# Gate and up products of the second layer's FFN as seven products of quarters, with sums of quarters on VectorE and GpSimd

## The chip, the cores and the metric

The kernel runs on one core of a Trainium2 chip. TensorE multiplies, VectorE (DVE), ScalarE (ACT) and GpSimd (POOL) work on tiles in SBUF and PSUM, and SyncE (SP) issues the DMAs. The metric is the device time of one execution in microseconds, median of the runs shown.

## The reference

Two layers of a backbone over 1024 latent tokens (and 256 context tokens in the first), width 1024, in float32. Each layer mixes tokens in two ways (A and B, then C and D), and then runs a feed-forward part (FFN) on the normed tokens:

```python
def swiglu(h, w_gate, w_up, w_down):
    return (jax.nn.silu(h @ w_gate) * (h @ w_up)) @ w_down
...
        x = x + g_m * y
        x = x + g_f * swiglu(modulate(rmsnorm(x, norm_ffn_w[i]), sh_f, sc_f), ffn_w_gate[i], ffn_w_up[i], ffn_w_down[i])
```

The hidden width is 2816. A last rmsnorm gives the output. The change concerns `h @ w_gate` and `h @ w_up` of the second layer, for 1024 tokens.

## The kernel before

Float32 precision comes from three products of rounded operands: `split` (L54) makes a high part (a CAST on ScalarE, L56) and a low part (a subtraction on VectorE or GpSimd, L57), and `mm3` (L46) multiplies high by high, high by low, low by high into one PSUM bank, lines L49, L50, L51. Every matmul here is 128 x 128 weights by 512 tokens.

Tokens lie along the free axis: eight tiles `xT` of 128 channels by 1024 tokens hold x, and `mixc`, `mixd` hold the normed h, one high and one low tile for each of the eight depths. Tokens are taken in two blocks of 512 (`XBLK`).

Before the FFN, `out_proj` (L389) multiplies the mixed heads by the output weights, block by block, in four groups of two channel tiles (`op`), and `residual` (L312, one VectorE operation at L316) adds them to x. Behind each block, `rstd` (L264) squares x on ScalarE, sums on VectorE (`sqacc`, L275), sums over partitions on TensorE (`ss`, L279) and takes the root (`rv`, with a power on GpSimd, L249); `spread` (L253) makes a diagonal and spreads it by a matmul (`rbc`, L261); `norm` (L283) scales each channel tile (`nt`, L295), adds the shift and splits it, the odd tiles with GpSimd (L299 to L301), the even ones without (L303, L304).

`ffn` (L327) goes over 22 tiles of 128 hidden columns. `up` multiplies h by a gate tile and an up tile for one block (`pg`, `pu`, both named pg in the profile: 8 depths x 3 matmuls each), takes silu on ScalarE (L345), multiplies on VectorE (L346) and splits the hidden values. `down` takes two hidden tiles and multiplies them by the down weights into eight channel tiles and two blocks (`dn`, 16 x 6 matmuls), each added to x by `residual`. Down runs two tiles behind up. Weights come by DMA in slabs of 512 KB and are split (`wslab`, L60).

PSUM has eight banks. `psum` (L70) hands out tag "s" as halves of a tile of two banks, two such tiles in turn; the first and the second half of one tile go to two products that follow each other. The framework holds a writer of the second half back until the readers of the first half that stand ahead of it in the program are done. The down products of layer 2 use the four single banks of tags t, t, m and o.

The order of instructions on each engine is fixed when the kernel is built, by the framework's scheduler; pools with a number of buffers decide when a tile can be written again. At the end, `final` (L1294) norms each token, and the output is stored.

Of the kernel before, what the change touches and what calls it, by code (L numbers as in the profile page):

```python
# [53 lines left out]
def split(s, hi, lo, src, eng="act"):  # L54

    s.nc.scalar.copy(hi, src)  # L56
    (s.nc.gpsimd if eng == "pool" else s.nc.vector).tensor_tensor(lo, src, f32(hi), ALU.subtract)  # L57
# [12 lines left out]
def psum(s, tag, name=None):  # L70

    if tag != "s":
        return s.ps.tile([P, 512], F32, name=name or tag, tag=tag, bufs=2 if tag == "t" else 1)
# [187 lines left out]
    s.nc.tensor.matmul(bc[:, :n * P], s.ones, dg, start=True, stop=True)  # L261


def rstd(s, xT, blk, add=None):  # L264

    nc = s.nc
    o, n = blk
    acc = s.np_.tile([P, 512], F32, name="sqacc", tag="sqacc", bufs=2)
    for k in range(KT):
        if k == 0:  # L270
            nc.scalar.activation(acc[:, :n], xT[0][:, o:o + n], AF.Square)
        else:
            sq = s.np_.tile([P, 512], F32, name="sq", tag="sq", bufs=2)
# [1 line left out]
            (add or nc.vector).tensor_tensor(acc[:, :n], acc[:, :n], sq[:, :n], ALU.add)  # L275
# [1334 lines left out]
```

## Time and profile before

| what | value |
|---|---|
| median of 3 runs | 2867.76 us (2862.70 to 2868.23) |
| profiled execution | 2863.98 us, its span 2862.0 us |
| TensorE busy in the span | 2758.1 us, 96% |
| VectorE, ScalarE, GpSimd busy | 1551.5, 892.2, 196.5 us |
| last matmul of out_proj starts at | 2120.05 us |
| first gate product of layer 2 starts at | 2121.35 us |

A row of the timeline gives the start and the duration in us, the engine, the line of the kernel, the operation, what it writes and reads, and in brackets how long the engine was idle ahead of it and what ended that. Matmuls overlap in the pipeline, so a row of 0.39 us does not mean that the next starts 0.39 us later. PEld is the loading of weights. A row of a window gives its bounds and length, then busy time and number of instructions of PE, PEld, DVE, ACT and POOL, then the granted TensorE clock, the DMA share and GB/s.

### The profile page before, as it was taken

How to read it: one execution, taken by the hardware profiler on the slowest of the kernel's cores; microseconds unless marked ns; L12 is line 12 of the kernel's file. 1: busy time of each engine (PE TensorE's matmuls, PEld its weight loads, DVE VectorE, ACT ScalarE, POOL GpSimd, SP SyncE). 2: the span in 40 equal slices, each digit the busy share in tenths (PEclk: the TensorE clock that was granted, in tenths of full speed). 3: DMA queues.
4: the chain of work that ended last, by engine and by line, in shares of the span. 5: the costliest groups of instructions: out<-in, count | busy, mean ns of one | idle time of the engine just before them, and what ended most of it. 6: DMA issues, size and time to landing. Idle time of an engine off the chain costs nothing.

```text
span 2862.0 us, 38369 instructions
## 1 busy us (share of the span) xinstructions
PE 2758.1 (96%) x14927; PEld 2339.4 (82%) x14927; DVE 1551.5 (54%) x2791; ACT 892.2 (31%) x1899; POOL 196.5 (7%) x233
## 2 busy tenths in 40 slices
PE   8999999899999999999999998998999999999998
PEld 3889888777888888888888787787878888888887
DVE  4655677676664544645533466756673333333435
ACT  3432566554411111111111145654251111111112
POOL 0000222121100000000000020312010000000000
PEclk9999999999999999999999999999999999999999
DMA  8545655674231322313310143533631111111111
GB/s 302 169 129 154 183 156 171 207 215 129 70 115 59 97 65 61 103 39 95 89 37 30 46 148 100 164 118 102 213 101 52 45 45 52 52 45 52 52 45 67
DMA packets 285686, 298.50 MB, mean 104 GB/s; under 512 B 33416, under 2 KB 228673, under 8 KB 285505
## 3 DMA queue, kind: packets, MB, share of 16 engines
q1 hardware_dynamic: 285505, 296.06, 34.3%
q8 instruction: 118, 1.93, 0.3%
q14 instruction: 63, 0.52, 0.1%
HBM read 228.09 MB, written 64.49 MB: 102 GB/s over the span
## 4 chain that ended last, share of the span: by engine, by line
PE 79%; DVE 9%; DMA 5%; ACT 4%; issue 3%; POOL 1%; SPq 0%; DVEq 0%; ACTq 0%; POOLq 0%
PE pg L51 12%; PE pg L50 12%; PE pg L49 12%; PE dn L49 5%; PE dn L50 5%; PE dn L51 5%; PE o L750 2%; PE pt L720 1%; DMA adaw<-in_ada_w_dram 1%; DVE xT L316 1%; DVE adaacc L183 1%; DVE wlo L57 1%; PE ho L49 1%; PE sp L661 1%; PE qk L49 1%
## 5 line engine op out<-in xcount | busy, mean ns | idle before, releaser
L56 ACT CAST whi<-wraw 128x1024 fp32r<-128x1024 f32 (+2 forms) x186 | 188.4, 1014 | 676.4 <-PE dn L50 404.0
L316 DVE SCALAR_TENSOR_TENSOR xT<-dn,mod,xT 128x512 f32<-128x512 f32 (+1 forms) x448 | 299.7, 686 | 122.4 <-PE dn L51 120.3
L57 DVE TENSOR_TENSOR wlo<-wraw,whi 128x1024 fp32r<-128x1024 f32 (+2 forms) x186 | 220.7, 1189 | 238.2 <-ACT whi L56 236.4
L49 PE MATMUL dn<-hhi,whi 128*128 128x512 f32 (+1 forms) x896 | 328.6, 368 | 6.3 <-DVE xT L316 4.7
L50 PE MATMUL dn<-hlo,whi 128*128 128x512 f32 (+1 forms) x896 | 326.9, 365 | 0.0
L51 PE MATMUL dn<-hhi,wlo 128*128 128x512 f32 (+1 forms) x896 | 326.5, 365 | 0.0
L51 PE MATMUL pg<-hh,wlo 128*128 128x512 f32 x688 | 269.2, 391 | 0.6 <-DVE wlo L57 0.6
L49 PE MATMUL pg<-hh,whi 128*128 128x512 f32 x688 | 269.0, 391 | 0.0
L346 DVE TENSOR_TENSOR sg<-sg,pg 128x512 f32<-128x512 f32 (+1 forms) x110 | 69.3, 630 | 367.6 <-ACT sg L345 367.5
L50 PE MATMUL pg<-hl,whi 128*128 128x512 f32 x688 | 268.3, 390 | 0.0
L183 DVE SCALAR_TENSOR_TENSOR adaacc<-adaw,cs,adaacc 128x1024 f32<-128x1024 f32 x140 | 175.0, 1280 | 117.7 <-DMA adaw<-in_ada_w_dram 114.9
L345 ACT ACTIVATE sg<-pg 128x512 f32<-128x512 f32 (+1 forms) x110 | 60.6, 551 | 547.0 <-PE pg L51 547.0
L49 PEld LDWEIGHTS dn<-hhi,whi 128*128 128x128 f32 x896 | 168.9, 189 | 39.6 <-DVE xT L316 11.1
L51 PEld LDWEIGHTS dn<-hhi,wlo 128*128 128x128 f32 x896 | 168.9, 189 | 27.0
L50 PEld LDWEIGHTS dn<-hlo,whi 128*128 128x128 f32 x896 | 169.0, 189 | 26.3
L51 PEld LDWEIGHTS pg<-hh,wlo 128*128 128x128 f32 x688 | 129.5, 188 | 28.4 <-DVE wlo L57 1.5
L50 PEld LDWEIGHTS pg<-hl,whi 128*128 128x128 f32 x688 | 129.5, 188 | 26.0
L49 PEld LDWEIGHTS pg<-hh,whi 128*128 128x128 f32 x688 | 129.5, 188 | 25.9
L49 PE MATMUL pg<-mixc,whi 128*128 128x512 f32 x344 | 133.9, 389 | 0.9 <-DVE xT L316 0.9
L50 PE MATMUL pg<-mixd,whi 128*128 128x512 f32 x344 | 134.3, 390 | 0.0
L51 PE MATMUL pg<-mixd,wlo 128*128 128x512 f32 x344 | 133.8, 389 | 0.0
L50 PE MATMUL pg<-mixc,whi 128*128 128x512 f32 x344 | 133.8, 389 | 0.0
(569 smaller groups left out, 6198.7 us busy)
## 6 DMA issues: line engine op xcount, KB each, us to landing
adaw<-in_ada_w_dram SPq DMA_DIRECT2D x96, 512.0 KB, 3.9
wraw<-in_ffn_w_gate_dram SPq DMA_DIRECT2D x44, 512.0 KB, 3.7
wraw<-in_ffn_w_up_dram SPq DMA_DIRECT2D x44, 512.0 KB, 3.8
wraw<-in_ffn_w_down_dram SPq DMA_DIRECT2D x44, 512.0 KB, 3.8
wraw<-in_ab_w_in_dram SPq DMA_DIRECT2D x20, 512.0 KB, 6.3
xd<-xT SPq DMA_DIRECT2D x16, 640.0 KB, 6.1
xs<-xd SPq DMA_DIRECT2D x32, 256.0 KB, 3.2
xd<-xs SPq DMA_DIRECT2D x32, 256.0 KB, 2.9
```

The lines of the kernel that those rows point to most:

```text
L49: nc.tensor.matmul(out, wh, xh, start=start, stop=False)
L50: nc.tensor.matmul(out, wh, xl, start=False, stop=False)
L51: nc.tensor.matmul(out, wl, xh, start=False, stop=stop)
L56: s.nc.scalar.copy(hi, src)
L57: (s.nc.gpsimd if eng == "pool" else s.nc.vector).tensor_tensor(lo, src, f32(hi), ALU.subtract)
L183: nc.vector.scalar_tensor_tensor(acc[:, v], w, c, acc[:, v], ALU.mult, ALU.add)
L316: s.nc.vector.scalar_tensor_tensor(xT[k][:, o:o + n], ps, s.mod[l][:, 8 * vec + k, sel:sel + 1], xT[k][:, o:o + n], ALU.mult, ALU.add)
L345: nc.scalar.activation(sg[:, :n], pg[:, :n], AF.Silu)
L346: nc.vector.tensor_tensor(sg[:, :n], sg[:, :n], pu[:, :n], ALU.mult)
L661: nc.tensor.matmul(sp[:, o:o + n], qq[:, x, :], kk[:, t0:t0 + n], start=x == 0, stop=x == 1)
L720: nc.tensor.transpose(pt[:n, jj * P:(jj + 1) * P], y[:, c:c + n], s.ident)
L750: nc.tensor.matmul(o_ps[:, ba * P:bz * P], vv[:n, kt, :], at(x, sl)[:n, 0, ba:bz, :].rearrange("p b q -> p (b q)"), start=q == 0 and x == ...
```

## The change

Take h as four quarters: A11 is block 0 with the first four depths, A12 block 0 with the last four, A21 and A22 the same of block 1. Take the weights of two neighbouring hidden tiles as quarters B11, B12, B21, B22 (depth half by tile). Then the four quarters of the product come from seven products:

- sums of h: s1 = A21 + A22, s2 = s1 - A11, s3 = A11 - A21, s4 = A12 - s2, made once. `norm_first` keeps A11 and A11 + A12 in float32, and `norm_second`, the norm of block 1, makes the sums depth by depth.
- sums of weights: t1 = B12 - B11, t2 = B22 - t1, t3 = B22 - B12, and B21 - t2, made on GpSimd for each pair of tiles (`quarters`, L490); all seven are split.
- products (`quad`): 1 = A11 B11, 2 = A12 B21, 5 = s1 t1, 6 = s2 t2, 7 = s3 t3, 3 = s4 B22, 4 = A22 (B21 - t2), each of 4 depths x 3 matmuls.
- sums of products: c11 = 1 + 2; u = 1 + 6; c12 = u + 5 + 3; u + 7; c22 = u + 7 + 5; c21 = u + 7 + 4. Products 1 and 5 are copied from PSUM by ScalarE (L531, L536), 2, 6, 7, 3, 4 are added by VectorE (L533, L535, L539, L543, L546), and two sums of SBUF tiles are on GpSimd (L538, L541).

`ffn_sums` runs gate, then up, then down for each pair of hidden tiles, with down directly behind its pair. The weights' pool is closed and opened anew ahead of the FFN, with units of 4 x 128 columns; the pool of `norm_second`'s scratch is closed there, and the buffers `hu` of `quad` lie in its memory. The final norm's tiles come from a pool that takes the place of the sums.

```diff
-        norm(s, xT, hT, l, 1, blk, rstd(s, xT, blk), True)
+        behind(blk)
...
+        out_proj(s, a["cd_w_out"][0], mix, xT, 1, XBLK, [0, 1, 2, 3], S.places(),
+                 lambda blk: (norm_first if blk == XBLK[0] else norm_second)(s, xT, hT, S, 1))
...
-        ffn(s, a, 1, xT, hT, XBLK, TAIL, final(s, s.np_, a, xT, out))
+    wps.close()
+    with R("wp2") as s.wp, R("fp2") as s.fp:
...
+        ffn_sums(s, a, 1, xT, hT, S, tail)
```

The norm of block 1 with the sums, L455 to L478 (`normed` scales on VectorE, L431, and adds the shift on ScalarE, L432):

```python
    for k in range(4):
        a21, a22 = scratch(s), scratch(s)
        normed(s, xT, k, blk, bc, l, a21)
        normed(s, xT, k + 4, blk, bc, l, a22)
        s1 = sum_(nc.vector, a21, a22, ALU.add)
        s2 = sum_(nc.vector, s1, S.a11[k], ALU.subtract)
        s3 = sum_(nc.gpsimd, S.a11[k], a21, ALU.subtract)
        s4 = sum_(nc.gpsimd, S.a1s[k], s1, ALU.subtract)
        for i, v, eng in ((6, s2, "dve"), (5, s1, "dve"), (7, s3, "pool"), (3, s4, "dve"), (4, a22, "pool")):
            parts(i, k, v, eng)
```

The weights, L503 to L513, where `parts` splits a unit, and the products, L530 to L547, of which `out` names the place and `done` is silu for gate, multiplication (L572) and split for up:

```python
    sub(t, t, b11)
    parts(1, b11)
    parts(2, b21)
    parts(5, t)
    sub(t, b22, t)
    parts(6, t)
    sub(b21, b21, t)
    sub(t, t, b11)
    parts(7, t)
    parts(3, b22)
    parts(4, b21)
...
    u, v = room(), room()
    nc.scalar.copy(u, product(1))
    c = out(0, 0, None)
    add(c, product(2), u, ALU.add)
    done(0, 0, c)
    add(u, product(6), u, ALU.add)
    nc.scalar.copy(v, product(5))
    c12 = out(0, 1, None)
    nc.gpsimd.tensor_tensor(c12, u, v, ALU.add)
    add(u, product(7), u, ALU.add)
    c = out(1, 1, v)
    nc.gpsimd.tensor_tensor(c, u, v, ALU.add)
    done(1, 1, c)
    add(c12, product(3), c12, ALU.add)
    done(0, 1, c12)
    c = out(1, 0, u)
    add(c, product(4), u, ALU.add)
    done(1, 0, c)
```

How the instructions move is shown at three places. The first is TensorE at the norm of block 1 (ss and rbc are its two sums). Before, they stand within the gate products of the first tile:

```order
L50 MATMUL pg<-mixd,whi 128x512
L51 MATMUL pg<-mixd,wlo 128x512
L49 MATMUL pg<-mixd,whi 128x512
L279 MATMUL ss<-ones,sqacc 128x1 x4
L50 MATMUL pg<-mixd,whi 128x512
L51 MATMUL pg<-mixd,wlo 128x512
L49 MATMUL pg<-mixd,whi 128x512
L50 MATMUL pg<-mixd,whi 128x512
L51 MATMUL pg<-mixd,wlo 128x512
```

After, product 1 (mixc) ends, then come both, and directly behind them product 6, whose operands s_19651, s_19678 and two more are s2 of the four depths:

```order
L51 MATMUL qp<-mixc,wlo 128x512
L279 MATMUL ss<-ones,sqacc 128x1 x4
L261 MATMUL rbc<-diag,ones 128x512
L49 MATMUL qp<-s_19651,whi 128x512
L50 MATMUL qp<-s_19651,whi 128x512
L51 MATMUL qp<-s_19651,wlo 128x512
L49 MATMUL qp<-s_19678,whi 128x512
L50 MATMUL qp<-s_19678,whi 128x512
L51 MATMUL qp<-s_19678,wlo 128x512
```

So no product stands beside the sums: the 12 matmuls of product 1 are ahead of ss, and product 2, which needs nothing of block 1, stands behind product 6.

The second place is VectorE and GpSimd in the norm of block 1. VectorE before, from its first scaling on (L295, nt are scaled tiles, mixc the low parts at L304):

```order
L295 SCALAR_TENSOR_TENSOR nt_19630<-xT0_19241,acol11_182,rbc_19626 128x512
L295 SCALAR_TENSOR_TENSOR nt_19634<-xT1_19242,acol11_182,rbc_19626 128x512
L304 SCALAR_TENSOR_TENSOR mixc_18359<-nt_19630,mod1_178,mixc_18358 128x512
L295 SCALAR_TENSOR_TENSOR nt_19639<-xT2_19243,acol11_182,rbc_19626 128x512
L295 SCALAR_TENSOR_TENSOR nt_19643<-xT3_19244,acol11_182,rbc_19626 128x512
L304 SCALAR_TENSOR_TENSOR mixc_18799<-nt_19639,mod1_178,mixc_18798 128x512
L346 TENSOR_TENSOR sg_19745<-sg_19745,pg_19696 128x512
```

VectorE after, depth 0 and the beginning of depth 1 (nt_19637 and nt_19638 are a21 and a22 of depth 0, nt_19643 is s1, nt_19645 s2, nt_19649 s4; L463 are sums, L57 low parts):

```order
L431 SCALAR_TENSOR_TENSOR nt_19637<-xT0_19241,acol11_182,rbc_19633 128x512
L431 SCALAR_TENSOR_TENSOR nt_19638<-xT4_19245,acol11_182,rbc_19633 128x512
L463 TENSOR_TENSOR nt_19643<-nt_19637,nt_19638 128x512
L463 TENSOR_TENSOR nt_19645<-nt_19643,s30_19438 128x512
L57 TENSOR_TENSOR mixc_18359<-nt_19643,mixc_18358 128x512
L431 SCALAR_TENSOR_TENSOR nt_19664<-xT1_19242,acol11_182,rbc_19633 128x512
L57 TENSOR_TENSOR s20_19651<-nt_19645,s20_19651 128x512
L57 TENSOR_TENSOR s40_19659<-nt_19649,s40_19659 128x512
L431 SCALAR_TENSOR_TENSOR nt_19665<-xT5_19246,acol11_182,rbc_19633 128x512
L463 TENSOR_TENSOR nt_19670<-nt_19664,nt_19665 128x512
L463 TENSOR_TENSOR nt_19672<-nt_19670,s31_19439 128x512
```

GpSimd in the same stretch had only the low parts of four odd tiles before; after, a depth reads:

```order
L57 TENSOR_TENSOR mixd_18286<-nt_19638,mixd_18285 128x512
L463 TENSOR_TENSOR nt_19647<-s30_19438,nt_19637 128x512
L463 TENSOR_TENSOR nt_19649<-s40_19442,nt_19643 128x512
L57 TENSOR_TENSOR s30_19656<-nt_19647,s30_19656 128x512
L57 TENSOR_TENSOR mixd_18288<-nt_19665,mixd_18287 128x512
L463 TENSOR_TENSOR nt_19674<-s31_19439,nt_19664 128x512
```

The scaling of a22 of depth 1 (nt_19665) has come to stand behind the low part of s4 of depth 0 (s40_19659), which needs GpSimd's third operation of that depth.

The third place is TensorE inside a pair of tiles, at gate's products 7, 4 and 3. Before, at the border of two tiles (pg_20240 is the up product of block 1, pg_20308 the PSUM tile that gate and up of the next tile's block 0 share, matmul by matmul):

```order
L49 MATMUL pg_20240<-mixd_18291,whi_20182 128x512
L50 MATMUL pg_20240<-mixd_18292,whi_20182 128x512
L51 MATMUL pg_20240<-mixd_18291,wlo_20183 128x512
L49 MATMUL pg_20308<-mixc_18358,whi_20298 128x512
L50 MATMUL pg_20308<-mixc_18359,whi_20298 128x512
L51 MATMUL pg_20308<-mixc_18358,wlo_20299 128x512
L49 MATMUL pg_20308<-mixc_18358,whi_20304 128x512
L50 MATMUL pg_20308<-mixc_18359,whi_20304 128x512
L51 MATMUL pg_20308<-mixc_18358,wlo_20305 128x512
```

After, in the third pair of tiles (qp_20743 is a PSUM tile of two banks with product 7 in its first half and product 3 in its second, qp_20775 the next one):

```order
L49 MATMUL qp_20743<-s33_19737,whi_20671 128x512
L50 MATMUL qp_20743<-s33_19737,whi_20671 128x512
L51 MATMUL qp_20743<-s33_19737,wlo_20672 128x512
L49 MATMUL qp_20775<-mixd_18285,whi_20679 128x512
L50 MATMUL qp_20775<-mixd_18286,whi_20679 128x512
L51 MATMUL qp_20775<-mixd_18285,wlo_20680 128x512
L49 MATMUL qp_20775<-mixd_18287,whi_20679 128x512
L49 MATMUL qp_20743<-s40_19659,whi_20675 128x512
L50 MATMUL qp_20743<-s40_19659,whi_20675 128x512
L51 MATMUL qp_20743<-s40_19659,wlo_20676 128x512
```

A product that had begun ran to its end before, alone or with its partner; now four matmuls of product 4 have come to stand between the end of product 7 (s33) and the beginning of product 3 (s40), which writes the second half of product 7's tile. The other products of a pair lie in the same way: another product's first 4 to 6 matmuls, then the second half.

More of the change, by code (lines that the diff above doesn't have):

```diff
@@ L261, in spread, with rstd @@
     s.nc.tensor.matmul(bc[:, :n * P], s.ones, dg, start=True, stop=True)
-def rstd(s, xT, blk, add=None):
+def rstd(s, xT, blk, add=None, tag=None, bufs=2):
     nc = s.nc
     o, n = blk
-    acc = s.np_.tile([P, 512], F32, name="sqacc", tag="sqacc", bufs=2)
+    acc = s.np_.tile([P, 512], F32, name="sqacc", tag=tag or "sqacc", bufs=bufs)
     for k in range(KT):
@@ L386, in ffn, with __init__, new, places @@
     down(HT - 2, hs[HT - 2:])
-def out_proj(s, w, mix, xT, hT, l, blocks, order, places):
+class Sums:
+    def __init__(self, pool):
+        self.pool = pool
+        self.s = {}
+    def new(self, tag, shape=(P, 2, 512), dt=F32R):
+        return self.pool.tile(list(shape), dt, name=tag, tag=tag, bufs=1)
+    def places(self):
+        for i in (0, 2):
+            yield [self.new(f"s2{i + x}", (P, 4, 2 * P)) for x in range(2)]
+    def first(self):
+        return [[self.new(f"s{i}{k}", dt=F32)[:, 0, :] for k in range(4)] for i in (3, 4)]
+    def operand(self, hT, i, k):
+        if i in (6, 7, 3):
+            tag = f"s{ {6: 2, 7: 3, 3: 4}[i]}{k}"
+            if tag not in self.s:
+                self.s[tag] = self.new(tag)
+            return self.s[tag][:, 0, :], self.s[tag][:, 1, :]
+        k0, o = {1: (0, 0), 2: (4, 0), 4: (4, 512), 5: (0, 512)}[i]
+        return [hT[k0 + k][x][:, o:o + 512] for x in range(2)]
@@ new lines, with scratch, normed, spread_rstd @@
+SCRATCH = 8
+def scratch(s):
+    return s.np_.tile([P, 512], F32, name="nt", tag="nt", bufs=SCRATCH)
+def normed(s, xT, k, blk, bc, l, dst):
+    o, n = blk
+    s.nc.vector.scalar_tensor_tensor(dst, xT[k][:, o:o + n], s.acol[l][1][:, k, 0:1], bc[:, :n], ALU.mult, ALU.mult)
+    s.nc.scalar.activation(dst, dst, AF.Identity, bias=s.mod[l][:, 24 + k, 0:1])
+def spread_rstd(s, xT, blk):
+    r = rstd(s, xT, blk, None, "nt", SCRATCH)
+    bc = psum(s, s.nbanks[1], "rbc")
+    spread(s, s.np_, r, bc, "nt", SCRATCH)
+    return bc
@@ new lines, in norm_first, with norm_second, sum_, parts @@
+def norm_first(s, xT, hT, S, l):
+    blk = XBLK[0]
+    bc = spread_rstd(s, xT, blk)
+    S.a11, S.a1s = S.first()
+    for k in range(KT):
+        v = (S.a11 if k < 4 else S.a1s)[k % 4]
+        normed(s, xT, k, blk, bc, l, v)
+        split(s, hT[k][0][:, :512], hT[k][1][:, :512], v, "pool" if k % 2 else "dve")
+        if k >= 4:
+            s.nc.gpsimd.tensor_tensor(v, v, S.a11[k - 4], ALU.add)
+def norm_second(s, xT, hT, S, l):
+    nc = s.nc
+    blk = XBLK[1]
+    bc = spread_rstd(s, xT, blk)
+    def sum_(e, x, y, op):
+        out = scratch(s)
+        e.tensor_tensor(out, x, y, op)
+        return out
+    def parts(i, k, v, eng):
+        split(s, *S.operand(hT, i, k), v, eng)
+    for k in range(4):
+        a21, a22 = scratch(s), scratch(s)
[7 more added lines that the diff above has]
+            parts(i, k, v, eng)
@@ new lines, in unit, with quarters, parts @@
+def unit(s):
+    return [s.wp.tile([P, 4, P], F32R, name=f"w{x}", tag=f"w{x}", bufs=4) for x in ("hi", "lo")]
+def quarters(s, w, j):
+    sub = lambda out, x, y: s.nc.gpsimd.tensor_tensor(out, x, y, ALU.subtract)
+    raw = []
+    for x in range(2):
+        raw.append(s.wp.tile([P, 4, 2 * P], F32, name="wraw", tag="wraw", bufs=2))
+        s.nc.sync.dma_start(raw[x], w[512 * x:512 * (x + 1), j * P:(j + 2) * P].rearrange("(k p) n -> p k n", p=P))
+    b11, t, b21, b22 = [r[:, :, P * y:P * (y + 1)] for r in raw for y in range(2)]
+    ops = {}
+    def parts(i, src):
+        hi, lo = unit(s)
+        split(s, hi, lo, src)
+        ops[i] = [(hi[:, k, :], lo[:, k, :]) for k in range(4)]
+    sub(t, t, b11)
[9 more added lines that the diff above has]
+    parts(4, b21)
+    return ops
@@ new lines, in quad, with product @@
+def quad(s, ws, xs, room, out, done):
+    nc = s.nc
+    add = nc.vector.tensor_tensor
+    def product(i):
+        ps = psum(s, "s", "qp")
+        for k in range(4):
+            mm3(nc, ps, ws[i][k], xs[i][k], k == 0, k == 3)
+        return ps
+    u, v = room(), room()
[16 more added lines that the diff above has]
+    done(1, 0, c)
@@ L392, in out_proj @@
+def out_proj(s, w, mix, xT, l, blocks, order, places, behind):
     q0, nq = min(order), len(order)
@@ L1498, in body @@
             with R("np1") as s.np_:
-                out_proj(s, a["ab_w_out"][0], mix, xT, hT, 0, BLK, [4, 5, 6, 7], hidden(s, (P, 4, 2 * P)))
+                out_proj(s, a["ab_w_out"][0], mix, xT, 0, BLK, [4, 5, 6, 7], hidden(s, (P, 4, 2 * P)),
+                         lambda blk: norm(s, xT, hT, 0, 1, blk, rstd(s, xT, blk), True))
             dump("x1", xT)
```

61 lines of the change are left out of this document (56 added, 5 removed).

## The prediction

> **What bounds the kernel now.** I read the engine totals first, then the stretch that the change touches (from the first gate product of layer 2 to the end), then its groups on TensorE.
>
> ```profile
> span 2862.0 us, 38369 instructions
> PE 2758.1 (96%) x14927; PEld 2339.4 (82%) x14927; DVE 1551.5 (54%) x2791; ACT 892.2 (31%) x1899; POOL 196.5 (7%) x233
> ```
> ```profile
> 2121.00:2862.00 741.00, 730.57 (x3290) 605.72 (x3290) 291.30 (x390) 140.26 (x202) 11.53 (x14) 0.99 0.16 49
> ```
> ```profile
> L49 PE MATMUL dn<-hhi,whi 128*128 128x512 f32 (+1 forms) x368 | 140.3, 381 | 0.0
> L49 PE MATMUL pg<-mixc,whi 128*128 128x512 f32 x344 | 133.9, 389 | 0.9 <-DVE xT L316 0.9
> ```
>
> In those 741.0 us TensorE is busy 730.6 at a granted clock of 0.99, VectorE 291, ScalarE 140, GpSimd 11.5. The last column of the groups is idle time ahead of them: 0.0 in front of the down products, 0.9 in front of the gate products, all of it once, at their start. So the stage is TensorE's alone: a matmul less is time less, and any wait that appears on TensorE is paid in full, since nothing there waits today.
>
> The price of a matmul, and the delays between engines, come from the timeline at one hand-over in that stage:
>
> ```profile
> 2168.45 0.39 PE L51 MATMUL pg<-mixd,hlo 128*128 128x512 f32 x1
> 2168.93 0.60 ACT L345 ACTIVATE sg<-pg 128x512 f32<-128x512 f32 x1 [4.67 <-PE pg L51]
> 2169.56 0.69 DVE L346 TENSOR_TENSOR sg<-sg,pg 128x512 f32<-128x512 f32 x1 [4.05 <-ACT sg L345]
> 2171.17 0.39 PE L51 MATMUL pg<-mixc,wlo 128*128 128x512 f32 x1
> ```
>
> Twelve matmuls lie between 2168.45 and 2171.17: 0.2267 us each. A reader starts 0.48 after the start of the last matmul it needs; one read of a PSUM half takes 0.60 on ScalarE, 0.69 on VectorE; the next engine starts 0.03 after that.
>
> **What the change removes.** Gate and up are 22 tiles x 2 matrices x 2 blocks x 8 depths x 3 = 2112 matmuls before, and 11 pairs x 168 (two matrices x 7 products x 4 depths x 3) = 1848 after. 264 x 0.2267 = **59.9 us** less, 5.4 a pair of tiles. All of it was on the path. The weight bytes stay the same, and the down products and the final norm keep their matmuls.
>
> **What it adds off the path.** Per pair of tiles VectorE gets 10 adds (6.9 us) and splits 14 weight units of 512 columns instead of 4 slabs of 1024 (14 x 0.69 for 4 x 1.22, rows below), ScalarE gets 4 copies of 0.60 and more casts, GpSimd 12 tensor operations of 1.30. TensorE needs 168 + 96 matmuls, 59.8 us, for a pair; in the window the three were at 39%, 19% and 2% of the time, so with some 12, 7 and 16 us more a pair none of them becomes the bound. They matter only by waits, of two kinds.
>
> **Cost 1, the head.** Before, block 1 is normed while TensorE multiplies block 0, so its length costs nothing. After, every product but the first two needs block 1, and the scheduled order puts product 6 (the sum s2, all four depths) behind product 1; product 2 comes third. So TensorE has 12 matmuls to do (2.7 us), then waits for the norm and its sums.
>
> ```profile
> 2120.05 0.39 PE L51 MATMUL op<-mixc,hlo 128*128 128x512 f32 x1
> 2121.35 0.47 PE L49 MATMUL pg<-mixc,whi 128*128 128x512 f32 x1 [0.91 <-DVE xT L316]
> ```
> ```profile
> 2123.96 4.67 DVE L275 TENSOR_TENSOR sqacc<-sqacc,sq 128x512 f32<-128x512 f32 x6
> 2133.04 1.41 DVE L295 SCALAR_TENSOR_TENSOR nt<-xT,acol,rbc 128x512 f32<-128x512 f32 x2 [1.22 <-PE rbc L261]
> 2141.55 0.69 DVE L57 TENSOR_TENSOR hlo<-sg,hhi 128x512 fp32r<-128x512 f32 x1
> 2142.93 0.75 DVE L295 SCALAR_TENSOR_TENSOR nt<-xT,acol,rbc 128x512 f32<-128x512 f32 x1
> ```
> ```profile
> 2141.66 0.72 ACT L299 ACTIVATE nt<-nt,mod 128x512 f32<-128x512 f32 x1 [0.92 <-DVE nt L295]
> 2142.42 0.62 ACT L300 CAST mixd<-nt 128x512 fp32r<-128x512 f32 x1
> ```
> ```profile
> 2106.92 1.97 POOL L301 TENSOR_TENSOR mixc<-nt,mixc 128x512 fp32r<-128x512 f32 x1 [5.66 <-ACT mixc L300]
> 2135.99 1.30 POOL L301 TENSOR_TENSOR mixc<-nt,mixc 128x512 fp32r<-128x512 f32 x1 [4.90 <-ACT mixc L300]
> ```
>
> Start of the norm of block 1: 2133.04 before, 4.41 after the last sqacc ended (2128.63). After, the last four residuals stand on VectorE behind the low parts of four weight units, one of which waits for a GpSimd subtraction with ten GpSimd operations of 1.30 ahead of it since the norm of block 0 began to use it (2106.92): 2106.92 + 13 = 2119.9, + CAST 0.62 + low part 0.69, then the residuals and the eight squares as before, and one more unit (0.69) ahead of the last sqacc: 2134.6 without contention, **2136** taken, 2133 to 2138 as bounds.
>
> One depth k of the sums: the bias (0.72) on a22, its CAST (0.62), three GpSimd operations in a row (low part of a22, s3, s4: 3.90), the CAST of s4 (0.62), its low part on VectorE (0.69), and only behind that the scaling of a22 of the next k (0.75): 7.3, with hand-overs **7.4 us** a depth. That is if VectorE and GpSimd do not disturb each other. The GpSimd operation at 2106.92 took 1.97 where the one at 2135.99 took 1.30; this row of VectorE says what it met:
>
> ```profile
> 2106.51 1.22 DVE L57 TENSOR_TENSOR wlo<-wraw,whi 128x1024 fp32r<-128x1024 f32 x1
> ```
>
> A VectorE operation with both inputs in SBUF held it up for 0.67 of the 0.81 that they overlap, while the operation at 2135.99 had only one-PSUM-input work beside it. A depth has five such VectorE operations (3.45) and four on GpSimd (5.20); taking turns they need **8.65**, which I take. The Trainium skill says, in SBUF — State Buffer, section "Who interferes with whom", that a VectorE instruction with two SBUF inputs and a GpSimd instruction that reads SBUF lock each other out for the whole instruction; this trace agrees (1.97 against 1.30), and taken strictly it makes the third rival.
>
> Product 6 ends 5.9 after three depths (28 to 32 from the start). Product 2 must wait for the copy of product 1, whose buffer takes memory of the norm's scratch and so waits for GpSimd's last operation: three depths (26.0) + 2.2 (scaling and bias) + 0.62 + four GpSimd operations (5.2 to 6) + copy 0.6 = 35 from the start, at 2171. Without any of this, product 2 would start at 2120.28 + 24 x 0.2267 = 2125.7. So 45.3 us of wait; minus the 1.07 that the first product waits in before (2121.35 against 2120.28); plus 1.1 where the first matmul of product 7 stands behind the add of product 2 (0.43 + 0.69 + 0.06 + 0.14, less one matmul; the terms are worked out below). And the clock: after the one long pause in before,
>
> ```profile
> 1775.98 0.80 PE L49 MATMUL gqk<-hh,whi 128*128 128x512 f32 x1 [4.31 <-ACT q L870]
> 1776.57 0.63 PE L50 MATMUL gqk<-hl,whi 128*128 128x512 f32 x1
> 1777.00 0.63 PE L51 MATMUL gqk<-hh,wlo 128*128 128x512 f32 x1
> ```
> ```profile
> 1775.90:1777.90 2.00, 1.92 (x5) 1.53 (x6) 2.00 (x2) 0.03 (x1) 0.00 (x0) 0.50 0.95 313
> 1779.90:1781.90 2.00, 2.00 (x10) 1.68 (x9) 2.00 (x3) 0.21 (x1) 2.00 (x1) 1.00 0.45 70
> ```
>
> matmuls come 0.43 apart at a granted clock of 0.50, and at 1.00 some 4 us later: eight matmuls late by 0.2 each, 1.7. **Head: 47 us**; 42 with depths of 7.4 and a start at 2135.
>
> **Cost 2, waits in each pair of tiles.** Two products share one PSUM tile of two banks, and its second half may not be written before the reader of the first half is done. That dependence is in before too, in the last down products of layer 1:
>
> ```profile
> 1634.16 0.39 PE L51 MATMUL dn<-hhi,wlo 128*128 128x512 f32 x1
> 1634.59 1.41 DVE L316 SCALAR_TENSOR_TENSOR xT<-dn,mod,xT 128x512 f32<-128x512 f32 x2 [1.68 <-PE dn L51]
> 1635.39 0.50 PE L49 MATMUL dn<-hhi,whi 128*128 128x512 f32 x1 [0.39 <-DVE xT L316]
> 1638.80 0.50 PE L49 MATMUL dn<-hhi,whi 128*128 128x512 f32 x1 [0.39 <-DVE xT L316]
> ```
>
> There the twelve matmuls from 1635.39 to 1638.80 take 3.41 instead of 2.72, a loss of 0.69, with two other matmuls between the halves. The chain is 0.43 to the read, 0.74 (half of the 1.41, with its overlap), 0.06 to the weights and 0.14 to the pace: 1.37, less 3 x 0.2267. In after the scheduler puts 4 to 13 matmuls between. With the same rule: product 2 behind the copy of 1 (1.26 - 5 x 0.2267) 0.13; product 5 behind the add of 6, up's product 1 behind gate's add of 4, up's product 6 behind its add of 2, 0.19 each; up's 7 behind the copy of 5, 0 to 0.3. Two chains are long. Gate's product 3 waits for the add of product 7, which waits for GpSimd's sum c12, which waits for the copy of product 5: 0.48 + 0.60 + 1.35 + 0.05 + 0.69 + 0.20 = 3.4, and a weight CAST (0.62) may stand ahead of the copy; 13 x 0.2267 = 2.95 run beside: 0.4 to 0.9. Up's product 4 waits for the add of 3, queued on VectorE behind a multiplication that waits for GpSimd's c11: 0.43 + 0.69 + 1.40 + 0.69 + 0.66 + 0.20 = 4.1, less 14 x 0.2267: 0.9. The first down products wait for the split of the last quarter, some 0.2. Together 2.2 to 3.0; GpSimd's two links stretch by up to 0.67 each when they meet VectorE's splits (22 low parts of 0.69 in 60 us, weights and hidden values, a quarter of the time). **2.9 a pair** taken, 10.5 pairs (the first gate quad lies in the head): 30.5.
>
> **Sum.** -59.9 + 47 + 30.5 = +17.6. The span goes from 2862.0 to 2879.6. The profiled execution took 2863.98, 3.8 under the median of the runs shown (2867.76); the difference added to the median gives **2885**.
>
> **The rivals.**
> Faster: the waits between halves are covered. If copies and adds start as promptly as at 2168.93 with no CAST ahead and the two GpSimd chains are met by the matmuls beside them, 0.5 a pair is left; with the short head that is -59.9 + 42 + 5 = -13, 2855. It decides at (59.9 - 47) / 10.5 = 1.2 us a pair. For it: 4 to 13 matmuls between against two in layer 1. Against: the two chains with GpSimd come out at 0.4 to 0.9 each by rows without any disturbance. 0.18.
> No change: depths of 7.4 and 1.7 a pair: -59.9 + 42 + 18 = 0, 2868. For it: the low ends of both costs. Against: the 1.97. 0.15.
> Slower still: GpSimd and VectorE block each other at every turn. Then on the chain of a depth the low part of s4 also waits out the low part of s3 (1.30 more than 7.4) and the three GpSimd operations wait for two VectorE ones (1.4 more): 10.1, the head is 53 with the late start, and a pair loses 4: -59.9 + 53 + 42 = +35, 2903. For it: 0.67 of 0.81 in the one clean meeting. Against: only a quarter of VectorE's time in the loop is such work. 0.09. Another way to the same place is the clock: if the small waits of a pair set it to half once, that costs 1.7 each time by the rows at 1775.98, 18 in 10.5 pairs: 2885 + 18 = 2903. Against: layer 1's waits come every 3.4 us (1635.39, 1638.80) and the matmuls between them keep their pace (2.72 of the 3.41). 0.03. The Trainium skill describes this in TensorE: Matmul & The Clock Gate, "A second HAM failure mode: psum-queue depth-cycling": frequent small pauses between groups of matmuls make the clock swing to half.
> That the saving is not there is out: the scheduled order has the 1848 matmuls, with the same operands as before in shape and type.
>
> **How the numbers follow.** My forecast has 0.55, with 2874 to 2896 as its own range (head 41 to 50, 2.4 to 3.4 a pair). A measurement of this kernel can tell 0.2% from no change, 5.7 us. Faster by more than that holds the first rival and a little of the second: 0.19; the same, 0.14; slower 0.67. The range reaches to the middle of the first rival and to the last: 2855 to 2904.
>
> **What would show it.** In the profile after: TensorE idle from about 2123 to 2171 but for a few matmuls, in front of s2 and of product 2, with the granted clock at half there; groups of the products with idle time behind VectorE's adds (L535, L539, L543) and the copies of 0.1 to 1 us, 2 to 3.5 us a pair; 1848 products at 0.2267. Wrong would be: the head under 35 us, because the scheduled order lets product 2 go earlier than I read; idle time under 1.2 a pair; or GpSimd operations of 1.30 throughout the sums, or well over 2.

## The result, and the profile after

The changed kernel takes 2898.26 us (median of 4 runs, 2897.97 to 2902.01) against 2865.27 us before (4 runs, 2862.70 to 2868.23): a ratio of 1.0118, 95% interval 1.0100 to 1.0135. It is slower by 33.0 us where 17.6 were forecast.

The totals of the page, and three windows of the stretch that the change touches (as before: bounds, length, then busy time and count of PE, PEld, DVE, ACT, POOL, the granted clock, DMA share, GB/s):

```profile
span 2899.9 us, 38795 instructions
PE 2732.8 (94%) x14663; PEld 2287.1 (79%) x14663; DVE 1706.3 (59%) x3049; ACT 982.2 (34%) x2095; POOL 407.2 (14%) x381
```
```profile
2121.00:2162.00 41.00, 14.31 (x43) 8.47 (x42) 29.64 (x33) 16.94 (x28) 19.20 (x15) 0.65 0.04 13
2162.00:2200.00 38.00, 24.37 (x81) 17.15 (x82) 22.05 (x22) 13.78 (x23) 17.94 (x13) 0.71 0.05 14
2200.00:2862.00 662.00, 639.55 (x2722) 502.54 (x2722) 372.74 (x539) 188.59 (x312) 171.24 (x123) 1.00 0.16 51
```

TensorE has 264 matmuls less, as counted. In the first window it runs 43 matmuls in 41 us, 173 in the same window before, and its clock is at 0.65. From 2200 on the clock is full, and 22.5 us are idle; before, 8.7 were idle in the same window, 8.6 of them behind 2850, in the last norm. TensorE's waits by what ended them (total, times, longest) from 2115 on:

```profile
PE qp L49 <- ACT s L56: 20.8, 4, 5.5
PE qp L49 <- DVE hlo L543: 10.8, 11, 1.0
PE qp L50 <- DVE s L57: 7.6, 4, 1.9
PE qp L51 <- DVE wlo L57: 5.3, 10, 0.5
PE ss L279 <- DVE sqacc L275: 4.8, 1, 4.8
PE qp L49 <- DVE hu L539: 4.3, 11, 0.6
PE rbc L261 <- DVE diag L258: 3.1, 1, 3.1
PE dn L50 <- DVE hlo L57: 2.5, 10, 0.3
```

Waits that come four times or once belong to the head; those that come ten or eleven times come once in a pair of tiles.

**The head.** TensorE, rows picked from the timeline:

```profile
2111.59 0.47 PE L49 MATMUL op<-mixc,s 128*128 128x512 f32 x1 [3.19 <-ACT mixd L56]
2125.75 0.47 PE L49 MATMUL qp<-mixc,whi 128*128 128x512 f32 x1 [1.38 <-ACT sqacc L271]
2146.11 0.80 PE L49 MATMUL qp<-s,whi 128*128 128x512 f32 x1 [5.50 <-ACT s L56]
2155.15 0.79 PE L49 MATMUL qp<-s,whi 128*128 128x512 f32 x1 [5.13 <-ACT s L56]
2178.17 0.80 PE L49 MATMUL qp<-mixd,whi 128*128 128x512 f32 x1 [1.13 <-ACT hu L531]
2178.76 0.63 PE L50 MATMUL qp<-mixd,whi 128*128 128x512 f32 x1
2179.19 0.63 PE L51 MATMUL qp<-mixd,wlo 128*128 128x512 f32 x1
```

Product 1 starts at 2125.75, product 6 takes its three matmuls of a depth every 9.0 us, and product 2 starts at 2178.17, with its matmuls 0.43 apart from the second on. VectorE and GpSimd in the same stretch, the first depth and the beginning of the second:

```profile
2140.64 1.40 DVE L431 SCALAR_TENSOR_TENSOR nt<-xT,acol,rbc 128x512 f32<-128x512 f32 x2 [2.17 <-PE rbc L261]
2143.62 1.78 DVE L463 TENSOR_TENSOR nt<-nt,s 128x512 f32<-128x512 f32 x1
2152.67 1.78 DVE L463 TENSOR_TENSOR nt<-nt,s 128x512 f32<-128x512 f32 x1
```
```profile
2143.59 1.27 POOL L57 TENSOR_TENSOR mixd<-nt,mixd 128x512 fp32r<-128x512 f32 x1 [5.66 <-ACT mixd L56]
2144.81 3.39 POOL L463 TENSOR_TENSOR nt<-s,nt 128x512 f32<-128x512 f32 x2
```

The sum s2 at 2143.62 started 0.03 after GpSimd and took 1.78 instead of 0.69; GpSimd's next two took 1.70 each instead of 1.27. Both engines stretch, and the next depth follows 9.05 us later (2152.67).

**A pair of tiles.** One pair, from the first down product of the second pair to that of the third, and the longer waits behind it, rows of TensorE picked from the timeline; then the first two down products of the kernel before:

```profile
2277.62 0.39 PE L49 MATMUL dn<-hhi,whi 128*128 128x512 f32 x1
2341.80 0.39 PE L49 MATMUL dn<-hhi,whi 128*128 128x512 f32 x1
2344.31 0.50 PE L49 MATMUL qp<-mixd,whi 128*128 128x512 f32 x1 [0.98 <-DVE hlo L543]
2347.81 0.50 PE L50 MATMUL dn<-hlo,whi 128*128 128x512 f32 x1 [0.26 <-DVE hlo L57]
2372.21 0.50 PE L51 MATMUL qp<-s,wlo 128*128 128x512 f32 x1 [0.53 <-DVE wlo L57]
2384.38 0.50 PE L49 MATMUL qp<-s,whi 128*128 128x512 f32 x1 [0.37 <-DVE hu L539]
```
```profile
2190.43 0.39 PE L49 MATMUL dn<-hhi,whi 128*128 128x512 f32 x1
2255.71 0.39 PE L49 MATMUL dn<-hhi,whi 128*128 128x512 f32 x1
```

A pair takes 64.18 us (64.13 to 64.23 over ten). Before it was 65.28, which is 288 x 0.2267 and no wait at all; 264 x 0.2267 would be 59.85. So of the 5.43 us saved in a pair, 4.3 are given back. What a wait costs is the distance of the matmul's start from the start before it, less 0.2267, and 0.11 more at the next one: 1.26 at 2344.31 (up's product 4), 0.54 at 2347.81 (down), 0.81 at 2372.21 (weights of gate's product 6), 0.64 at 2384.38 (gate's product 3); six more of 0.09 to 0.18 have no idle time in the view, since a matmul's row is longer than the distance to the next.

### The profile page after: what moved, and what is told of

It reads as the page before. It is cut to its first block, busy times and chain, and to the rows that moved or that the text cites. A ratio compares the mean times of both kernels' runs of the same rounds, so it can differ in the third digit from the quotient of the medians.

```text
span 2899.9 us, 38795 instructions
## 1 busy us (share of the span) xinstructions
PE 2732.8 (94%) x14663; PEld 2287.1 (79%) x14663; DVE 1706.3 (59%) x3049; ACT 982.2 (34%) x2095; POOL 407.2 (14%) x381
## 4 chain that ended last, share of the span: by engine, by line
PE 66%; DVE 12%; issue 9%; DMA 5%; ACT 5%; POOL 3%; SPq 0%; DVEq 0%; POOLq 0%; ACTq 0%
PE pg L51 6%; PE pg L49 6%; PE pg L50 6%; PE qp L49 4%; PE qp L50 4%; PE qp L51 4%; PE dn L49 3%; PE dn L50 3%; PE dn L51 3%; DVE wlo L57 2%; PE o L968 2%; DMA adaw<-in_ada_w_dram 1%; DMA wraw<-in_ffn_w_gate_dram 1%; PE pt L938 1%; DVE adaacc L183 1%
## 5 line engine op out<-in xcount | busy, mean ns | idle before, releaser
L56 ACT CAST whi<-wraw 128x512 fp32r<-128x512 f32 (+2 forms) x319 | 243.0, 763 | 734.5 <-PE dn L50 391.9
L57 DVE TENSOR_TENSOR wlo<-wraw,whi 128x512 fp32r<-128x512 f32 (+2 forms) x319 | 289.0, 907 | 203.6 <-ACT whi L56 203.4
L490 POOL TENSOR_TENSOR wraw<-wraw 128x512 f32<-128x512 f32 x88 | 118.2, 1343 | 342.6 <-DVE wlo L57 250.8
L345 ACT ACTIVATE sg<-pg 128x512 f32<-128x512 f32 (+1 forms) x66 | 34.6, 524 | 353.3 <-PE pg L51 353.3
L346 DVE TENSOR_TENSOR sg<-sg,pg 128x512 f32<-128x512 f32 (+1 forms) x66 | 39.2, 594 | 186.8 <-ACT sg L345 186.8
L275 POOL TENSOR_TENSOR sqacc<-sqacc,sq 128x512 f32<-128x512 f32 (+1 forms) x14 | 17.0, 1218 | 901.1 <-ACT sq L274 900.0
L49 PE MATMUL qp<-s,whi 128*128 128x512 f32 x264 | 109.2, 414 | 26.0 <-ACT s L56 20.8
L56 ACT CAST hhi<-sg 128x512 fp32r<-128x512 f32 (+1 forms) x110 | 63.6, 578 | 164.5 <-DVE sg L346 94.9
```

Source lines behind the costliest of these rows:

```text
L49: nc.tensor.matmul(out, wh, xh, start=start, stop=False)
L345: nc.scalar.activation(sg[:, :n], pg[:, :n], AF.Silu)
L346: nc.vector.tensor_tensor(sg[:, :n], sg[:, :n], pu[:, :n], ALU.mult)
L490: sub = lambda out, x, y: s.nc.gpsimd.tensor_tensor(out, x, y, ALU.subtract)
```

## The experiments

All kernels ran beside runs of the kernel before on the same chip, whose median was 2865.27 us beside the changed kernel, 2868.65 beside e1 to e4, 2865.96 beside e5 to e8 and 2866.30 beside e9 and e10; the ratios allow for that, the times in us do not. The time at which the same early instruction runs differs from execution to execution (the first scaling of block 0 between 2098.2 and 2107.5 us), so stages are compared by their own length: the head from the first scaling of block 0 to the first down product, 111.4 us in the changed kernel and 87.2 before (a kernel that does more there), and the pair. Heads differ by some 1 us for no edit's sake: the part up to the first scaling of block 1, which e1 to e6 leave as it is, took 38.5 us in the changed kernel and 37.1 to 37.6 in those six.

| run | us, median | ratio to before (95%) | head | pair |
|---|---|---|---|---|
| changed | 2898.26 | 1.0118 (1.0100 to 1.0135) | 111.4 | 64.2 |
| e1 sums of h on VectorE | 2891.00 | 1.0085 (1.0068 to 1.0103) | 103.6 | 64.2 |
| e2 a bank for each product | 2887.37 | 1.0060 (1.0045 to 1.0076) | 106.0 | 62.3, 63.9 |
| e3 sums of products on VectorE | 2881.62 | 1.0046 (1.0031 to 1.0061) | 108.9 | 62.0 |
| e4 product 5 ahead of 6 | 2894.45 | 1.0094 (1.0077 to 1.0111) | 107.9 | 63.7 |
| e5 e1 and e3 | 2872.94 | 1.0023 (1.0013 to 1.0032) | 103.7 | 62.0 |
| e6 e5, two products, then readers | 2849.44 | 0.9943 (0.9930 to 0.9956) | 98.2 | 60.4 |
| e7 first pair plain | 2886.74 | 1.0077 (1.0062 to 1.0093) | 98.4 | 64.2 |
| e8 e6 and first pair plain | 2846.45 | 0.9926 (0.9909 to 0.9943) | 92.0 | 60.4 |
| e9 residual ahead | 2899.17 | 1.0109 (1.0090 to 1.0127) | 108.2 | 64.2 |
| e10 e8 and residual ahead | 2842.64 | 0.9916 (0.9900 to 0.9931) | 92.9 | 60.4 |

### e1: the sums of h on VectorE

```diff
-        s3 = sum_(nc.gpsimd, S.a11[k], a21, ALU.subtract)
-        s4 = sum_(nc.gpsimd, S.a1s[k], s1, ALU.subtract)
+        s3 = sum_(nc.vector, S.a11[k], a21, ALU.subtract)
+        s4 = sum_(nc.vector, S.a1s[k], s1, ALU.subtract)
...
-        for i, v, eng in ((6, s2, "dve"), (5, s1, "dve"), (7, s3, "pool"), (3, s4, "dve"), (4, a22, "pool")):
+        for i, v, eng in ((6, s2, "dve"), (5, s1, "dve"), (7, s3, "dve"), (3, s4, "dve"), (4, a22, "dve")):
```

> The changed kernel, but the sums s3 and s4 and the low parts of s3 and a22 in the norm of block 1 are on VectorE, so GpSimd has nothing to do there. Theory (the head is bound by the chain through both engines, stretched because VectorE operations with two SBUF inputs and GpSimd operations shut each other out): the depth falls from the 8.99 us of the changed kernel to what VectorE needs, 2 x 0.67 + 9 x 0.61 = 6.8 to 7.4 us, its two-input operations fall from 1.75 to 0.69 us each, product 6 comes about 7 us earlier, the total falls by 6 to 9 us. Rival (the head is bound by the number of steps between the engines, not by shutting out): a depth of 8.5 to 9 us as before and a total within 2 us of the changed kernel. The waits within a pair of tiles stay at 4.3 us in both.

VectorE, one sum and the two after it, and TensorE's first matmul of two depths:

```profile
2147.05 0.68 DVE L463 TENSOR_TENSOR nt<-nt,s 128x512 f32<-128x512 f32 x1
2147.65 1.29 DVE L463 TENSOR_TENSOR nt<-s,nt 128x512 f32<-128x512 f32 x2
```
```profile
2148.44 0.79 PE L49 MATMUL qp<-s,whi 128*128 128x512 f32 x1 [4.94 <-ACT s L56]
2156.16 0.79 PE L49 MATMUL qp<-s,whi 128*128 128x512 f32 x1 [5.35 <-ACT s L56]
```

s2 takes 0.68 instead of 1.78, a depth 7.7 us instead of 9.0 (6.8 to 7.4 were expected), and the head is 7.8 us shorter, 1.2 of it ahead of the sums. VectorE has nine operations with two SBUF inputs in a depth where it had five, and GpSimd none. So the help of GpSimd made the sums longer. The pair is as it was.

### e2: a bank for each product

The PSUM pool is closed ahead of the FFN and opened anew with four single banks for the products; the final norm takes two of them for each transposed tile.

```diff
+    pss.close()
+    s.ps = ctx.enter_context(P_("ps2", space=PSUM))
...
-        ps = psum(s, "s", "qp")
+        ps = psum(s, "q", "qp")
```

> The changed kernel, but each product has a PSUM bank of its own, four in turn, instead of halves of two tiles of two banks. Theory (a pair of tiles loses 4.3 us, about 2.9 of them because a second half waits for the reader of the first half and for what that reader waits for): the loss falls to 0.8 (weights of product 6) to 1.5 us a pair, 64.16 us to 60.7 to 61.4, and product 2 goes ahead of the sums in the head, 5 us earlier: the total falls by 33 us, to about that of the kernel before. Rival (the halves only show a wait that the buffers of the copies and the GpSimd sums would make anyway): the loss stays above 3 us a pair, the total falls by 5 to 15 us.

In the head the expectation was missed, because of the edit itself. TensorE, then VectorE:

```profile
2173.21 0.77 PE L49 MATMUL qp<-mixc,whi 128*128 128x512 f32 x1 [28.67 <-issue]
```
```profile
2172.27 0.73 DVE L431 SCALAR_TENSOR_TENSOR nt<-xT,acol,rbc 128x512 f32<-128x512 f32 x1
```

The first product waits until the last scaling has read rbc (2172.27 + 0.73): it is held back until that tile of the closed pool is read. Whether its bank lies over that of rbc was not looked at. In a pair the waits between halves are gone and the scheduler lays out product behind product, but down now starts directly behind product 4 and waits for the third quarter's split:

```profile
2278.67 0.73 PE L49 MATMUL dn<-hhi,whi 128*128 128x512 f32 x2 [2.11 <-ACT hhi L56]
...
2280.32 0.63 PE L49 MATMUL dn<-hhi,whi 128*128 128x512 f32 x1
2280.75 0.63 PE L50 MATMUL dn<-hlo,whi 128*128 128x512 f32 x1
```
```profile
2280.00:2283.40 3.40, 3.40 (x10) 2.63 (x9) 2.58 (x4) 0.59 (x1) 0.00 (x0) 0.50 0.44 124
```

That is 2.4 us and the only loss of most pairs (62.25); in four of ten, seven or eight matmuls behind it also run at half the clock, 0.43 apart (63.87). So the loss falls from 4.3 to 2.4, short of the 0.8 to 1.5 that the theory gave and of the rival's 3: the waits between halves are gone, and the chain through GpSimd to the hidden values comes out at the next place where TensorE needs it. Two links of that chain are a GpSimd sum of 1.67 (2271.31) and, on VectorE, the multiplication for the third quarter, 1.76 instead of 0.69 (2276.20) beside a GpSimd subtraction of weights.

### e3: the sums of products on VectorE

```diff
-    nc.gpsimd.tensor_tensor(c12, u, v, ALU.add)
+    add(c12, u, v, ALU.add)
...
-    nc.gpsimd.tensor_tensor(c, u, v, ALU.add)
+    add(c, u, v, ALU.add)
```

> The changed kernel, but the two sums of SBUF tiles in each group of seven products (c12 and c11 of the changed code) are on VectorE instead of GpSimd. Theory (GpSimd's 1.3 to 1.7 us is a link of the two long chains to gate's product 3 and up's product 4): these two waits fall by about 0.6 to 1 us each, a pair from 64.16 to 62.2 to 63 us, the total falls by 12 to 20 us. Rival (VectorE's own queue is what delays these chains): no change in the pair, or longer.

As the theory had it. The pair falls to 62.0, by 2.2 (62.2 to 63 were expected), and the waits behind L543 (10.8 us in all before) and L539 (4.3) are no longer in the view; the wait of down for its hidden values (2.5) goes with them. The one for weights (L57, 5.3) stays.

### e4: product 5 ahead of product 6

```diff
-    add(u, product(6), u, ALU.add)
     nc.scalar.copy(v, product(5))
+    add(u, product(6), u, ALU.add)
```

> The changed kernel with product 5 ahead of product 6. Theory (0.8 us a pair is a wait of gate's product 6 for its weights, whose subtraction overwrites a tile that the split of product 5's weights must have read, and that split waits for a unit that the down products still read): the wait for the low part goes, as product 6 comes 2.7 us later, and gate's product 3 waits less since its GpSimd sum has product 7 beside it: the pair falls from 64.16 to 62.7 to 63.4, the total by 8 to 14 us. Rival (the weights come late as a whole, the wait only moves to product 5): the pair stays within 0.4 us.

TensorE's waits of that kernel:

```profile
PE qp L49 <- DVE hlo L543: 11.2, 11, 1.3
PE qp L49 <- DVE hu L539: 8.3, 10, 0.8
```

The wait for weights is gone, as expected; the one of product 3 behind the add of product 7 nearly doubled from 4.3. That add waits for the GpSimd sum c12, which now stands behind VectorE's add of product 6, not behind a copy on ScalarE, and takes 1.68 us instead of 1.31, with a low part on VectorE beside it (2310.90 and 2310.74). The pair falls by 0.4 only. The weights were late by a time that 2.7 us of other work cover, but half of the gain went to the GpSimd chain: the rival's size, with another mechanism.

### e5: both on VectorE

The edits of e1 and e3 together.

> The changed kernel with both earlier edits: the sums of h and the sums of products all on VectorE, GpSimd only subtracts weights. Theory (head and pair are separate costs that add): a depth of 7.7 us as with the sums alone, a pair of 62.0 us as with the adds alone, the total 7 us under the 2881.6 of the adds alone, 2873 to 2877. Rival (VectorE becomes what the pair waits for, with 10.8 us more in a pair and no GpSimd beside it): a pair over 62.5 us or a total over 2880.

2872.94, the head as in e1 (103.7), the pair as in e3 (62.0): the two costs are separate and add. Moving GpSimd's sums to VectorE takes back 25 of the 33 us. Without it the saving and the waits nearly cancel, 1.0023.

### e6: two products, then their readers

```diff
+    p, q = product(1), product(2)
-    nc.scalar.copy(u, product(1))
+    nc.scalar.copy(u, p)
...
-    add(c, product(2), u, ALU.add)
+    add(c, q, u, ALU.add)
```

and the same for 6 with 5 and 7 with 3; product 4 has a tile of its own. Both sums are on VectorE as in e5.

> As the kernel with all sums on VectorE, but the seven products are written two at a time into the two halves of a PSUM tile, and only then read, so that no second half stands behind the reader of its first half. Theory (the small waits that are left, 0.1 to 0.2 us each, are this dependence): a pair falls from 62.0 to 60.2 to 61.2 us (0.4 to 1.4 us lost), and product 2 goes ahead of the sums in the head, which makes that 4 to 5 us shorter: a total of 2850 to 2862. Rival (a tile is now released only after both its readers, and the wait moves to the third pair of products): a pair of 62 us or more.

The group of down's first matmuls, x368, of this kernel and of the changed one (minimum, median and maximum in ns, then the first and last start):

```profile
L49 PE MATMUL dn<-hhi,whi x368: 278/389/497, 2202.8 to 2836.1; 128*128 128x512 f32 x168, 128*128 128x256 f32 x16
```
```profile
L49 PE MATMUL dn<-hhi,whi x368: 277/389/398, 2213.5 to 2888.2; 128*128 128x512 f32 x168, 128*128 128x256 f32 x16
```

633.3 us against 674.7 for ten pairs and the last down. A pair takes 60.37, 0.5 more than its matmuls. Product 2 now stands ahead of the sums, and the head falls by 5.5. This is 16 us faster than the kernel before.

### e7: the first pair of tiles plain

```diff
-        hs = up(j)
+        hs = up(j) if j else plain(j)
```

`plain` makes eight products, four of 24 matmuls for block 0 from A11 and A12, then four for block 1 from s1 and A22.

> The changed kernel, but the first pair of hidden tiles takes eight products: block 0 with A11 and A12, block 1 as s1 B11 + A22 (B21 - B11) and the same for the second column, so that 96 matmuls need nothing of block 1. Later pairs are as changed. Theory (the head costs what TensorE has no work for while block 1 is normed and summed): 84 more matmuls run beside the norm and the sums, 19 us, and 24 are added, the first down product comes 18 to 24 us earlier, the total is 2874 to 2882. Rival (TensorE waits there for something else, such as the weights or the memory of the norm's scratch, and the plain products only wait in turn): less than 8 us earlier. A pair stays at 64.2 us in both.

TensorE at the first product of block 1, and ScalarE there:

```profile
2175.91 0.79 PE L49 MATMUL qp<-mixc,whi 128*128 128x512 f32 x1 [28.27 <-ACT sg L637]
```
```profile
2174.78 1.08 ACT L637 ACTIVATE sg<-qp 128x512 f32<-128x512 f32 x2 [1.66 <-DVE s L57]
```

The head falls by 13.0, between the two expectations. Of that, 6.8 lie ahead of the first scaling of block 1 (31.8 us instead of 38.5), where the units of this pair need no subtraction on GpSimd and the clock is still full. The 96 matmuls do run beside the norm, but then both PSUM tiles are full, and the silu that would free them waits for the last low part of the sums (s at L57): its output lies in a pool opened in the place of the sums' scratch. So TensorE waits 28 us, for memory as the rival had it, in place of doing the part of block 1's products that is ready.

### e8: all of it

> All that the runs point to in one kernel: sums of h and of products on VectorE, two products then their readers, and the plain first pair. Theory (head, pair and clock costs add up, and nothing else stands against the saved matmuls): a pair of 60.2 to 61.2 us, the first down product near 2186 to 2192, a total of 2828 to 2845, faster than before by 20 to 40 us. Rival (the costs share a cause, so that their removal doesn't add): 2850 to 2868.

2846.45: 1.5 above the upper end that the theory gave, with the pair (60.4) and the first down product (2190.2) as expected. The head is 6.2 shorter than in e6, with the 24 matmuls that the plain pair has more, and in the profiled executions the whole stretch behind the first scaling of block 0 is 6.3 shorter (743.2 to 736.8). The medians differ by 3.0 only, which the intervals don't separate; the runs of e8 spread from 2836.84 to 2853.34, and the profiled one was the fastest.

### e9 and e10: the residuals ahead of block 0's last scalings

The last four depths of block 0's norm are issued behind the first group of block 1's output projection.

```diff
-    for k in range(KT):
+    ks(0, 4)
+    s.later = lambda: ks(4, KT)
```

> The changed kernel, but the last four depths of block 0's norm stand in the program behind the first group of block 1's output projection, so that VectorE takes that group's residuals ahead of them. From the first scaling of block 0 to the first of block 1 it is 29.8 us before and 38.5 us after. Theory (part of it is a chain: eight scalings run ahead, the residuals behind them hold the PSUM tiles that the projection's third group waits for, 3.2 us, and the matmuls behind that wait run at half the clock): the wait goes, the stretch falls to 33 to 35.5 us, the total by 3 to 6 us. Rival (the stretch is set by the weight units whose GpSimd subtractions stand ahead of the last residuals): the wait goes, but the stretch stays above 37 us and the total within 2 us.

The wait of 3.19 at 2111.59 is gone, product 1 comes 6.6 us earlier after the first scaling, and the stretch falls from 38.5 to 35.4 us (from 37.1 to 37.6 by e1 to e6). But the sums' start depends on the squares, and TensorE then waits for those instead:

```profile
PE ss L279 <- DVE sqacc L275: 9.5, 1, 9.5
```

The total is the same within its interval. So both hold in part: the residuals are one part of the longer stretch, and not the one that sets the time. What the remaining 5.6 us against before's 29.8 are was not tried singly. The last residuals still stand behind a weight unit that waits for GpSimd, 22.8 us after the first scaling of block 0 (22.2 in the changed kernel, 18.2 in e7).

> The kernel with all edits (sums on VectorE, two products then their readers, plain first pair) and the residuals of block 1's first group ahead as well. Theory: the first down product comes 3 to 6 us earlier than without this edit, counted from the first scaling of block 0; the pairs stay at 60.4 us; the total 2838 to 2845. Rival (TensorE has plain products beside the stretch, so its length is hidden now): within 1.5 us, 2845 to 2850.

The head is 92.9 against 92.0 without the edit: the rival, since the plain products cover that stretch. The total of 2842.64 lies in the theory's range instead, but it and the 2846.45 of e8 can't be told apart. e8 and e10 are the fastest, 0.993 and 0.992 of the kernel before.

## Why the prediction was right or wrong

**Direction and mechanism: right.** Slower, by an exposed head and by waits in each pair that together outweigh the saved matmuls. The saving of 5.4 us a pair is there: with nearly all waits gone (e6) a pair takes 60.4 against 65.3, 4.9 of it. The total of 2898 lies 2 us above the forecast's own range (2874 to 2896), and inside the whole range, up to 2904, only by the price of the slower rivals. The median of before had moved too, from the 2867.76 to which I added to 2865.27.

**Sizes: both costs were too small.** In the profiled executions the stretch from the first scaling of block 0 to the end grew by 39.0 us (758.8 to 797.8; the profiled execution of the changed kernel, 2902.01, was its longest). With the saving of 59.9 the losses are 98.9. Ten pairs at 4.3 are 43; forecast was 29 for them. The head and the first pair are 56; forecast was 48.5.

**The step that failed most is the sum for a pair, 2.9.** Of its parts, the small waits between halves came out about as worked out (0.09 to 0.18 against 0.13 to 0.19), and so did gate's product 3 (0.64, between 0.4 and 0.9). Up's product 4 took 1.26 instead of 0.9, the GpSimd link there being 1.67 as in the bound that I gave but did not take. Down's first products took 0.54 instead of 0.2. And one wait was not on the list: 0.81 for the weights of gate's product 6. Its chain in the changed kernel, ScalarE, VectorE, GpSimd:

```profile
2367.53 0.62 ACT L56 CAST whi<-wraw 128x512 fp32r<-128x512 f32 x1 [9.61 <-PE dn L50]
```
```profile
2368.18 0.69 DVE L57 TENSOR_TENSOR wlo<-wraw,whi 128x512 fp32r<-128x512 f32 x1 [0.43 <-ACT whi L56]
2370.93 1.23 DVE L57 TENSOR_TENSOR wlo<-wraw,whi 128x512 fp32r<-128x512 f32 x1 [1.39 <-ACT whi L56]
```
```profile
2368.95 2.66 POOL L490 TENSOR_TENSOR wraw<-wraw 128x512 f32<-128x512 f32 x2 [21.75 <-DVE wlo L57]
```

A unit of weights is free only when a down product has read it (2367.53), the split of t1 follows, and only then may GpSimd overwrite t1 with t2 (2368.95). The low part of t2, for which TensorE waits, then takes 1.23 instead of 0.69 (2370.93), beside GpSimd's next subtraction: 0.54 of the 0.81. I had counted the busy time of that work (16 us on GpSimd in 60) and concluded that it matters only by waits, and then listed no wait for weights. Four unit buffers and an operation in place were a chain too; more buffers were not tried.

**The head, 47.** The depth was 9.0 against 8.65, right in its reason: e1 shows that GpSimd's part costs 1.3 us a depth. The term that was mis-sized is the start of block 1's norm. From the first scaling of block 0 it came after 38.5 us, 29.8 before: 8.7 more, where I took 3, and 5 at most. The path was the one that I named, the last residuals behind a weight unit that waits for GpSimd, but not its lengths:

```profile
2102.10 2.06 DVE L431 SCALAR_TENSOR_TENSOR s<-xT,acol,rbc 128x512 f32<-128x512 f32 x3 [1.22 <-PE rbc L261]
2123.10 1.23 DVE L57 TENSOR_TENSOR wlo<-wraw,whi 128x512 fp32r<-128x512 f32 x1 [4.46 <-ACT whi L56]
2136.73 1.75 DVE L258 TENSOR_TENSOR diag<-ident,rv 128x512 f32<-128x512 f32 x1 [1.13 <-POOL rv L249]
```
```profile
2121.12 2.66 POOL L490 TENSOR_TENSOR wraw<-wraw 128x512 f32<-128x512 f32 x2
```

The ten GpSimd operations that I priced at 13 us took 16.4, from 2106.08 to the CAST at 2122.45: four of them took 1.73 to 1.83, and GpSimd was idle for 1.6 between the first ones. The low part behind that CAST took 1.23 instead of 0.69, and diag 1.75 instead of 0.69, as it met a GpSimd subtraction that had begun 0.06 earlier (in e1 to e6 it takes 0.69). And the clock fell to half at 2132.9, in the pause behind product 1, so that VectorE waited 1.96 for the sum over partitions (1.21 before) and 2.17 for the spread one (1.22 before). Together that is 3.4 + 0.5 + 1.1 + 1.7 = 6.7 us more than my sum without contention, of which I had allowed for 1.4. I had also not seen that with eight places for scaled tiles, instead of two, VectorE runs all eight scalings ahead of the residuals, and that the projection waits for their PSUM tile; e9 takes that wait away and shows that it sets some 2 of the 38.5.

**The rivals.** The faster one needed the two chains through GpSimd to be covered by the matmuls beside them; e3 shows that they are not. The slower one, 2903, was nearer in its total (2898) than the forecast and in the pair (4.0 against 4.3), but for other reasons than it gave: the depth was 9.0, not 10.1. The clock's part of it didn't occur in the changed kernel, whose ten pairs lie within 0.1 us of each other; it did in e2.

## What to carry to other kernels

A matmul saved on a saturated TensorE is saved in full only if every product's result is read in time: count the chains from a product's end to the next write of its PSUM tile, and of its weights' buffers, engine by engine, before counting busy time. Writing two products and then issuing their readers removed nearly all of the waits that were left here, and moving work from GpSimd back to a busier VectorE won more than the work cost. What an algebraic saving needs ahead of its first product must have other products beside it; here only two of seven had.

## What the runs showed of the hardware

- VectorE with two SBUF inputs and GpSimd stretch each other: 0.69 to 1.78 us and 1.27 to 1.70. The Trainium skill, SBUF — State Buffer, section "Who interferes with whom", calls it an exclusive lock, and in these rows VectorE lost 1.09 (1.78 - 0.69) of the 1.24 us that GpSimd's instruction still had to run, nearly all of it, while GpSimd lost 0.43 in each of its next two, less than the 0.69 of one VectorE instruction.
- The granted clock fell behind a wait of 2.1 us in e2, in four of ten equal places, for 3.4 us. In the trace's record of the clock the four falls are at 2279.96, 2406.25, 2593.99 and 2720.28, which is 37, 55 and 37 times 3.413 us apart, so they lie on a grid of that step. In those four places 1.96 to 2.11 us of the wait fall into the one step of the grid just ahead of the fall (2276.55 to 2278.67, for one); in the six others a boundary of the same grid cuts the wait, and at most 1.78 fall into one step (2340.43 to 2342.54 is cut at 2341.40). In the Trainium skill, TensorE: Matmul & The Clock Gate, the section "A second HAM failure mode: psum-queue depth-cycling" has short pauses do this; the waits of up to 1.0 us in the changed kernel's pairs did not.
- Closing a pool and opening another in its memory held the first writer back until a late reader of the old one was done; TensorE stood 28.7 us behind this in e2 (2173.21) and 28.3 in e7 (2175.91). Whether the two tiles lie over each other was not looked at.
